# Two gated projections of a decoder block: operand rows requested two groups before their split, additions moved to VectorE, half of the results gated once

## The chip, the cores and the metric

One core of a Trainium2 chip runs the whole program in one launch. The metric is device microseconds of one execution. TensorE (PE) multiplies, ScalarE (ACT) copies, VectorE (DVE) and GpSimd (POOL) work elementwise, SyncE (SP) issues the transfers (DMAs) to and from the chip's memory. Each engine takes its instructions strictly in order: one that waits holds all behind it.

## What is computed

```python
xn = rmsnorm(x, norm1_g[l])
qa, ka, va, qr, kr, vr, gr, gate_a, gate_b = [xn @ wl[:, bounds[i]:bounds[i + 1]] ...]
o_a = ...   # dilated attention, three groups mixed: (1, 1024, 512)
o_r = retention(...)
o_r = head_groupnorm(o_r, ...) * silu(gr)          # (1, 1024, 2048)
y = sigmoid(gate_a) * (o_a @ w_proj_a[l]) + sigmoid(gate_b) * (o_r @ w_proj_b[l])
x = x + y @ w_out[l]
x = x + square(relu(rmsnorm(x, norm2_g[l]) @ w_up[l])) @ w_down[l]
```

The sequence has 1024 rows, the model 1024 columns. The change concerns the end of the retention and the line of `y`: the two products and the two gates.

## The kernel before, in words

All numbers are float32. An operand is split into a high and a low part (`xh`, `xl`; for weights `wh`, `wl`): ACT copies the high part (L320), DVE subtracts it for the low part (L321), and each product of two operands is three matmuls, high by high, high by low, low by high. A group of 12 matmuls (four pieces of the inner dimension, three matmuls each) fills one tile of PSUM with 128x512 results, always issued at L223.

The stages that matter here follow each other on PE:

- **Retention**, four heads of eight chunks. Each chunk's output is normalised (L847 to L854), turned and multiplied by a gate (`turn_o`, L879 to L896); for the second half of the sequence POOL forms sums and differences of row blocks there (L893 to L896), and SP stores them all to `on_d` (L874). In the last four chunks `load_oa` (L802) brings the attention's output in and splits it.
- **The projection of the attention's output**, called `pa` below: 16 groups (eight column blocks `d`, two halves of the sequence), PSUM tile `ms`. A gate tile `s0` is loaded (L929, pool `pm2` of four buffers, three groups ahead), DVE multiplies it with the product (L957), SP stores it to `pa_d` (L958). After each group `load_sum` requests one 512 KB piece of rows of the next projection from `on_d` (L941, tile `oraw`, two buffers) and splits it at once.
- **The sevenfold projection of the retention's output**, called `pb`: eight units, the first four over one half of the inner dimension (c=0), the last four over the other (c=1). A unit computes a 2x2 block of results from seven products N1 to N7 in place of eight (Strassen's scheme), each a group of 12 matmuls; 56 groups in all, PSUM tiles `mm` and `ms`. Its weights are loaded by SP in raw form (L176), summed by DVE (L121) and split. Behind the products stand small steps: N1 is copied with its sign turned (L387, ACT), N6 is copied (L392, ACT), N7 is copied (L395, ACT) and the PSUM tile of N5 subtracted (L396, DVE), N3 is subtracted (L401, DVE). N2, N7, N4 and N3 each end in one result of 128x512, the blocks (0,0), (1,1), (1,0), (0,1) of (`f`, half of the sequence). In units 0 to 5 the order is N7, N4, N3, with products of unit j+2 between them; in units 6 and 7 N3 stands right behind N7 and uses the PSUM bank that L396 reads.
- Each result is multiplied by its gate (L1013, DVE; the gate loaded at L929 as `s1`) and added to what stands in memory (loaded at L929 as `s2`): POOL adds at L1015, L1018 or L1021, except in the last unit, where DVE adds. The added tile comes from `pa_d` in units 0 to 3 and from `pb_d` in units 4 to 7. Units 0 to 3 store to `pb_d` (L1016); units 4 to 7 split their results for the next projection (`keep`, L320/L321) or store them for later (L1022).
- Then the `w_out` projection, the up and the down projection.

What sets the order: the Python program writes all instructions in order, and a scheduler places them on the engines' queues by what they depend on and by when their buffers come free. So a load stands on SP where the program asks for it and its buffer has been released, and a split stands in ACT's and DVE's queue even where its load has not landed.

## Time and profile before

| what | value |
|---|---|
| time, median of 3 runs | 2283.23 us (2280.83 to 2285.7) |
| the profiled execution's own time | 2280.93 us |
| its span on the engines | 2279.2 us |
| mean granted TensorE clock | 0.992 |
| end of the retention, first group of `pa` on PE | 1302.7 us |
| `pa` on PE | 1302.7 to 1367.7 us |
| `pb` on PE | 1367.7 to 1547.6 us |

The span runs from the first to the last instruction of the trace, and all places in time are counted from its start. In the tables of windows each stretch has its length, then for each engine the busy time and the number of instructions, then the granted clock (1.00 is full), the busy share of the DMA engines and the rate. In the timeline a row has start, duration, engine, line, operation and tiles; the bracket at its end is the idle time of that engine before it, and what ended it.

### The profile page before, as it was taken

How to read it: one execution, taken by the hardware profiler on the slowest of the kernel's cores; microseconds unless marked ns; L12 is line 12 of the kernel's file. 1: busy time of each engine (PE TensorE's matmuls, PEld its weight loads, DVE VectorE, ACT ScalarE, POOL GpSimd, SP SyncE). 2: the span in 40 equal slices, each digit the busy share in tenths (PEclk: the TensorE clock that was granted, in tenths of full speed). 3: DMA queues.
4: the chain of work that ended last, by engine and by line, in shares of the span. 5: the costliest groups of instructions: out<-in, count | busy, mean ns of one | idle time of the engine just before them, and what ended most of it. 6: DMA issues, size and time to landing. Idle time of an engine off the chain costs nothing. (4 is left out here: it accounts for less than half of the span.)

```text
span 2279.2 us, 30618 instructions
## 1 busy us (share of the span) xinstructions
PE 2222.4 (98%) x10772; PEld 1898.7 (83%) x10772; DVE 1349.3 (59%) x2531; ACT 1044.1 (46%) x2330; POOL 444.8 (20%) x465
## 2 busy tenths in 40 slices
PE   8999999999999999999999989899999999899999
PEld 7999999998888888888888867677778888688777
DVE  6444545355544445558776756773765556687874
ACT  6444435345333333445555534342555555654542
POOL 1111111110000000002133112220000000587883
PEclk9999999999999999999999999999999999999999
DMA  4313132222233333264454388764345556645432
GB/s 151 95 52 112 56 94 93 82 84 98 88 111 111 111 111 109 100 190 126 116 148 124 118 269 290 264 220 145 118 120 152 153 152 191 221 153 180 163 133 102
DMA packets 248717, 313.74 MB, mean 138 GB/s; under 512 B 15218, under 2 KB 171250, under 8 KB 248563
## 3 DMA queue, kind: packets, MB, share of 16 engines
q1 hardware_dynamic: 248562, 311.79, 42.7%
q8 instruction: 84, 1.38, 0.2%
q14 instruction: 71, 0.57, 0.1%
HBM read 212.02 MB, written 99.71 MB: 137 GB/s over the span
## 5 line engine op out<-in xcount | busy, mean ns | idle before, releaser
L321 DVE TENSOR_TENSOR wl<-raw,wh 128x1024 fp32r<-128x1024 f32 (+2 forms) x290 | 321.6, 1112 | 361.5 <-ACT wh L320 360.6
L223 PE MATMUL mm<-wh,xh 128*128 128x384 f32 (+1 forms) x1226 | 481.7, 393 | 0.6 <-DVE Y L1252 0.5
L223 PE MATMUL mm<-wh,xl 128*128 128x384 f32 (+1 forms) x1226 | 438.8, 358 | 2.2 <-DVE xl L321 2.2
L223 PE MATMUL mm<-wl,xh 128*128 128x384 f32 (+1 forms) x1226 | 437.5, 357 | 0.0
L320 ACT ACTIVATE wh<-raw 128x1024 fp32r<-128x1024 f32 (+2 forms) x290 | 273.5, 945 | 350.6 <-PE ms L223 105.9
L223 PE MATMUL mm<-xh,wh 128*128 128x512 f32 x720 | 284.3, 395 | 18.0 <-ACT ms L387 8.5
L223 PE MATMUL ms<-xh,wh 128*128 128x512 f32 x700 | 277.8, 397 | 9.8 <-DVE s L957 9.2
L223 PE MATMUL mm<-xl,wh 128*128 128x512 f32 x720 | 283.1, 393 | 1.7 <-DVE xl L321 1.7
L223 PE MATMUL mm<-xh,wl 128*128 128x512 f32 x720 | 282.9, 393 | 0.0
L223 PE MATMUL ms<-xl,wh 128*128 128x512 f32 x700 | 274.0, 391 | 0.7 <-DVE xl L321 0.7
L223 PE MATMUL ms<-xh,wl 128*128 128x512 f32 x700 | 273.9, 391 | 0.0
L223 PEld LDWEIGHTS mm<-wh,xl 128*128 128x128 f32 x1226 | 230.7, 188 | 22.4 <-DVE xl L321 3.1
L223 PEld LDWEIGHTS mm<-wh,xh 128*128 128x128 f32 x1226 | 231.8, 189 | 19.9 <-DVE Y L1252 1.3
L223 PEld LDWEIGHTS mm<-wl,xh 128*128 128x128 f32 x1226 | 232.5, 190 | 16.6
L223 PEld LDWEIGHTS mm<-xh,wh 128*128 128x128 f32 x720 | 136.8, 190 | 49.5 <-ACT ms L387 10.0
L223 PEld LDWEIGHTS ms<-xh,wh 128*128 128x128 f32 x700 | 132.6, 189 | 41.0 <-DVE s L957 8.3
L223 PEld LDWEIGHTS mm<-xl,wh 128*128 128x128 f32 x720 | 136.9, 190 | 30.4 <-DVE xl L321 2.1
L223 PEld LDWEIGHTS mm<-xh,wl 128*128 128x128 f32 x720 | 136.8, 190 | 28.8
L223 PEld LDWEIGHTS ms<-xh,wl 128*128 128x128 f32 x700 | 132.2, 189 | 27.9
L223 PEld LDWEIGHTS ms<-xl,wh 128*128 128x128 f32 x700 | 132.4, 189 | 27.5 <-DVE xl L321 1.0
L852 POOL TENSOR_TENSOR st<-st,half 128x1 f32<-128x1 f32 x32 | 25.5, 798 | 647.9 <-DMA sr<-sr_d 489.1
L334 POOL TENSOR_TENSOR ssa<-ssa,half 128x2 f32<-128x2 f32 x96 | 66.5, 693 | 427.6 <-DVE ssa L333 404.7
(301 smaller groups left out, 3698.6 us busy)
## 6 DMA issues: line engine op xcount, KB each, us to landing
raw<-in_w_att SPq DMA_DIRECT2D x48, 384.0 KB, 3.8
raw<-in_w_up SPq DMA_DIRECT2D x32, 512.0 KB, 3.8
h_d<-s SPq DMA_DIRECT2D x64, 256.0 KB, 4.3
raw<-in_w_down SPq DMA_DIRECT2D x32, 512.0 KB, 3.9
oraw<-on_d SPq DMA_DIRECT2D x28, 512.0 KB, 5.4
s<-sg_d SPq DMA_DIRECT2D x48, 256.0 KB, 3.9
xh<-h_d SPq DMA_DIRECT2D x11, 896.0 KB, 4.5
xl<-h_d SPq DMA_DIRECT2D x10, 896.0 KB, 4.7
```

What stands on the lines that cost most here:

```text
L223: self.nc.tensor.matmul(ps, x, y, start=start, stop=stop, skip_group_check=not first)
L320: nc.scalar.activation(dst_h, src, AF.Copy)
L321: nc.vector.tensor_tensor(dst_l, src, dst_h.bitcast(F), op=OP.subtract)
L334: nc.gpsimd.tensor_tensor(dst, dst, half[:, :w], op=OP.pow)
L852: nc.gpsimd.tensor_tensor(st[:, 9:10], st[:, 8:9], half[:, 0:1], op=OP.pow)
```

## The change

In units 0 to 3 results with `f == i` (N2 and N7) are no longer gated: N2 is copied out of PSUM by ACT (L1020), and both are stored to `pb_d` as they are. Their gating is done once in units 4 to 7, as (stored + new) times gate plus `pa`: three DVE instructions (L1025 to L1027) and three loads. The other two results of a unit keep the product with the gate and the addition, now both on DVE (L1029, L1030). So the 29 POOL additions go, and DVE's instructions for results go from 35 to 56; loads of 256 KB go from 32 to 16 in units 0 to 3 and from 32 to 40 in units 4 to 7.

`load_sum` now only requests its rows; the split (`part_sum`) is written two groups later. In `pa` a request is written every second group, in `pb` every group as long as fewer than two are under way. The first three gates and the first three requests are written at the end of the retention, for which their pools are opened inside it. There are 28 requests of rows before and after; 12 stand in `pa` before, 3 in the retention and 7 in `pa` after, where N4 of c=0 moves into `pb`. The results' tiles share one ring of seven buffers (before: three each of `s1` and `s2`). The new lines of the moved steps: split L320/L321 as before, row requests L786, gate loads L779, stores to `on_d` L894, to `pa_d` L963, gating in `pa` L962.

```diff
@@ -771,9 +771,29 @@
     gst.close()
 
 
+    SUMS = ("N1", "N2", "N5", "N4", "N7", "N3", "N6")
+    work = [(d, cs) for d in range(KT) for cs in halves()]
+
+    def loaded(from_, src, name):
+        t = from_.tile([P, 512], F, name=name)
+        nc.sync.dma_start(t, src)
+        return t
+
+    def load_sum(from_, c, name, h):
+
+        raw = from_.tile([P, 2, 512], F, name="oraw")
+        o = 2 * SUMS.index(name)
+        nc.sync.dma_start(raw, on_d[2 * c + h, o:o + 2].rearrange("k p t -> p k t"))
+        return raw
+
+    def part_sum(to, raw, h):
+
+        split(*(x[:, 2 * h:2 * h + 2] for x in to), raw)
+
...
-        cp = pool(ph, "cp2", 1)
+        comb, load = ExitStack(), ExitStack()
+        pc = pool(comb, "pc", 2)
...
         def load_oa(s):
-            raw = p2b.tile([P, S], F, name="oar", bufs=1)
+            raw = pr.tile([P, S], F, name="oraw")
...
-            St = cp.tile([P, 2, DV], F, name="St")
+            St = p2b.tile([P, 2, DV], F, name="St", bufs=1)
...
+                if (h, c) == (2, 1):
+                    comb.close()
+                    pr = pool(load, "pr", 3)
+                    pm2 = pool(load, "pm2", 4)
...
                 if h == RH - 1 and c >= 4:
                     load_oa(c - 4)
...
+                if h == RH - 1 and c == NT - 1:
+                    gates = [loaded(pm2, sg_d[0, d, :, cs], "s0") for d, cs in work[:3]]
+                    raws = [(name, g, load_sum(pr, 0, name, g), -3) for name, g in (("N5", 0), ("N5", 1), ("N7", 0))]
...
-        pr = pool(ph, "pr", 2)
-        load = ExitStack()
-        pm2 = pool(load, "pm2", 4)
-
...
-        gates = [loaded(pm2, sg_d[0, d, :, cs], "s0") for d, cs in work[:3]]
...
-        def load_sum(c, name, h):
-
-            raw = pr.tile([P, 2, 512], F, name="oraw")
-            o = 2 * SUMS.index(name)
-            nc.sync.dma_start(raw, on_d[2 * c + h, o:o + 2].rearrange("k p t -> p k t"))
-            xh, xl = OPB[c][name]
-            split(xh[:, 2 * h:2 * h + 2], xl[:, 2 * h:2 * h + 2], raw)
-
-        waiting = [(name, h) for name in ("N5", "N7", "N1", "N2", "N6", "N4") for h in range(2)]
...
-                if len(gates) < len(work):
-                    e, es = work[len(gates)]
-                    gates.append(loaded(pm2, sg_d[0, e, :, es], "s0"))
-                sga = gates[2 * d + (cs.start > 0)]
-                pp = ms.tile([P, 512], F, name="ms")
-                pipe.step(pp, [(uh[:, k * P:(k + 1) * P], ul[:, k * P:(k + 1) * P], oaS[k][0][:, cs], oaS[k][1][:, cs])
-                               for k in range(SLOTS)], {SLOTS - 1: lambda: W.free(ua)} if cs.start else None)
-                nc.vector.tensor_tensor(sga, sga, pp, op=OP.mult)
-                nc.sync.dma_start(pa_d[d, :, cs], sga)
...
-                if waiting and (ES or waiting[0][0] in OPB[0]):
-                    load_sum(0, *waiting.pop(0))
+        waiting = [("N7", 1)] + [(name, h) for name in ("N1", "N2", "N6") for h in range(2)]
+        for n, (d, cs) in enumerate(work):
+            if not cs.start:
+                ua, = W.take(1)
+                uh, ul = W[ua]
+            if len(gates) < len(work):
+                e, es = work[len(gates)]
+                gates.append(loaded(pm2, sg_d[0, e, :, es], "s0"))
+            pp = ms.tile([P, 512], F, name="ms")
+            pipe.step(pp, [(uh[:, k * P:(k + 1) * P], ul[:, k * P:(k + 1) * P], oaS[k][0][:, cs], oaS[k][1][:, cs])
+                           for k in range(SLOTS)], {SLOTS - 1: lambda: W.free(ua)} if cs.start else None)
+            nc.vector.tensor_tensor(gates[n], gates[n], pp, op=OP.mult)
+            nc.sync.dma_start(pa_d[d, :, cs], gates[n])
...
+            if raws and raws[0][0] in OPB[0] and raws[0][3] <= n - 2:
+                name, h, raw, _ = raws.pop(0)
+                part_sum(OPB[0][name], raw, h)
+            if waiting and waiting[0][0] in OPB[0] and n % 2 and len(raws) < 3:
+                name, h = waiting.pop(0)
+                raws.append((name, h, load_sum(pr, 0, name, h), n))
+        for name, h, raw, _ in raws:
+            part_sum(OPB[0][name], raw, h)
...
-        for h in range(2):
-            load_sum(0, "N3", h)
-            load_sum(1, "N1", h)
-
+        pr = pool(ph, "pr2", 2)
...
-        class parts:
-            @staticmethod
-            def tile(shape, dtype, name):
-                return pub.tile(shape, dtype, name=name, bufs=2 if name == "u2" else 1)
-
-        pm3 = pool(ph, "pm3", 3)
+        pm3 = pool(ph, "pm3", 7)
...
-            src = pa_d if j < 4 else pb_d
-            ahead[results[n]] = loaded(pm3, sg_d[1, d, :, cs], "s1"), loaded(pm3, src[d, :, cs], "s2")
+            if j < 4 and f == i:
+                return
+            srcs = [sg_d[1], pa_d] if j < 4 else [sg_d[1], pb_d] + [pa_d] * (f == i)
+            ahead[n] = [loaded(pm3, src[d, :, cs], "s") for src in srcs]
 
...
-            sgb, y = ahead.pop(results[n])
-            nc.vector.tensor_tensor(sgb, sgb, src, op=OP.mult)
+            if n not in ahead:
+                y = src
+                if src.space == PSUM:
+                    y = pm3.tile([P, 512], F, name="s")
+                    nc.scalar.activation(y, src, AF.Copy)
+                nc.sync.dma_start(pb_d[2 * j + f, :, cs], y)
+                return
+            sgb, y, *pa = ahead.pop(n)
+            if pa:
+                nc.vector.tensor_tensor(y, y, src, op=OP.add)
+                nc.vector.tensor_tensor(y, y, sgb, op=OP.mult)
+                nc.vector.tensor_tensor(y, y, pa[0], op=OP.add)
+            else:
+                nc.vector.tensor_tensor(sgb, sgb, src, op=OP.mult)
+                nc.vector.tensor_tensor(y, y, sgb, op=OP.add)
             if j < 4:
-                nc.gpsimd.tensor_tensor(y, y, sgb, op=OP.add)
                 nc.sync.dma_start(pb_d[2 * j + f, :, cs], y)
             elif f or cs.start:
-                (nc.vector if j == 7 else nc.gpsimd).tensor_tensor(y, y, sgb, op=OP.add)
                 keep(j, f, cs, y)
             else:
-                nc.gpsimd.tensor_tensor(y, y, sgb, op=OP.add)
                 nc.sync.dma_start(yl_d[j - 4], y)
 
...
-        todo, unit = [], {}
+        todo, unit = [(c, name, h) for c, name in ((0, "N4"), (0, "N3"), (1, "N1")) for h in range(2)], {}
...
-        for j, name in order:
-            product("pb", j, name, unit, OPB[j // 4], lambda: parts, result)
-            todo += [(new, h) for new in after.get((j, name), ()) for h in range(2)]
-            if todo:
-                load_sum(1, *todo.pop(0))
+        for i, (j, name) in enumerate(order):
+            product("pb", j, name, unit, OPB[j // 4], lambda: pub, result)
+            todo += [(1, after[j, name], h) for h in range(2) if (j, name) in after]
+            if begun and begun[0][0] <= i - 2:
+                _, c, op, h, raw = begun.pop(0)
+                part_sum(OPB[c][op], raw, h)
+            if todo and len(begun) < 2:
+                begun.append((i, *todo[0], load_sum(pr, *todo.pop(0))))
...
```

PE's rows stand in the same order before and after. Three places of the other queues follow; numbers behind names are those of buffers.

**SP in the middle of `pa`** (`pa_d` is the store of a gated result, `s0` the load of a gate, `oraw` the request of rows, `on_d` the stores of the last chunks of the retention). Before:

```order
L958 DMA pa_d_87<-s0_12843 128x512
L941 DMA oraw_13002<-on_d_85 128x2x512
L874 DMA on_d_85<-onE_12619 128x4x128
L929 DMA s0_13006<-sg_d_82 128x512
L874 DMA on_d_85<-onT_13023 128x4x128
L874 DMA on_d_85<-n6_13029 128x2x128
L176 DMA raw2_13044<-in_w_pb_q 128x1024
L958 DMA pa_d_87<-s0_12845 128x512
L941 DMA oraw_13066<-on_d_85 128x2x512
L958 DMA pa_d_87<-s0_12920 128x512
L929 DMA s0_13070<-sg_d_82 128x512
L941 DMA oraw_13087<-on_d_85 128x2x512
```

The same place after the change:

```order
L963 DMA pa_d_87<-s0_12842 128x512
L894 DMA on_d_85<-n6_12993 128x2x128
L894 DMA on_d_85<-onE_12526 128x4x128
L894 DMA on_d_85<-onT_12987 128x4x128
L779 DMA s0_13008<-sg_d_82 128x512
L963 DMA pa_d_87<-s0_12851 128x512
L894 DMA on_d_85<-onE_12626 128x4x128
L894 DMA on_d_85<-onT_13025 128x4x128
L894 DMA on_d_85<-n6_13031 128x2x128
L176 DMA raw2_13046<-in_w_pb_q 128x1024
L779 DMA s0_13072<-sg_d_82 128x512
L963 DMA pa_d_87<-s0_12924 128x512
```

The requests of rows between the gates and stores are gone from this stretch; the stores to `on_d` still stand between the gate loads.

**ACT in the last chunks of the retention** (`wh5` is a weight of `pa`, `vh`, `smh` and `Sh` belong to the retention's chunks, `on` is a chunk's output). Before:

```order
L320 ACTIVATE wh0_12733<-raw0_11932 128x512
L884 ACTIVATE onT_12719<-tr_12714,gng_105 128x128 x4
L320 ACTIVATE wh1_12764<-raw1_11960 128x512
L847 ACTIVATE on_12755<-ms_12745 128x512
L320 ACTIVATE Sh_12783<-St_11991 128x512
L320 ACTIVATE wh3_12792<-raw2_11985 128x512
L320 ACTIVATE Sh_12783<-St_11991 128x512
L320 ACTIVATE wh5_12817<-raw0_12737 128x512
L320 ACTIVATE vh_12823<-mm_12707 128x512
L320 ACTIVATE smh_12806<-sm_12804 128x128
```

After:

```order
L320 ACTIVATE wh0_12740<-raw0_11939 128x512
L320 ACTIVATE wh1_12771<-raw1_11967 128x512
L320 ACTIVATE xh_96<-oraw_12846 128x1024
L867 ACTIVATE on_12762<-ms_12752 128x512
L320 ACTIVATE xh_98<-oraw_12848 128x1024
L320 ACTIVATE Sh_12790<-St_11998 128x512 x2
L320 ACTIVATE wh3_12799<-raw2_11992 128x512
L320 ACTIVATE wh5_12824<-raw0_12744 128x512
L320 ACTIVATE vh_12830<-mm_12714 128x512
L320 ACTIVATE xh_98<-oraw_12968 128x1024
L904 ACTIVATE onT_12865<-tr_12860,gng_105 128x128 x2
L320 ACTIVATE smh_12813<-sm_12811 128x128
```

Four splits of requested rows (`xh<-oraw`) now stand between the chunks' steps, and `wh5` of `pa` stands ahead of `vh` and `smh` as before.

**ACT at unit 3 of `pb`** (L387 is the copy of an N1, L395 that of an N7, `wh` are weights). Before:

```order
L320 ACTIVATE xh_13064<-oraw_13905 128x1024
L320 ACTIVATE wh2_13887<-raw1_13661 128x1024
L392 ACTIVATE u2_13903<-ms_13627 128x512
L320 ACTIVATE xh_13064<-oraw_13922 128x1024
L320 ACTIVATE xh_96<-oraw_13941 128x1024
L387 ACTIVATE ms_13939<-mm_13926 128x512
L320 ACTIVATE wh5_13967<-raw0_13659 128x1024
L395 ACTIVATE u3_13957<-ms_13627 128x512
```

After:

```order
L320 ACTIVATE xh_13066<-oraw_13876 128x1024
L392 ACTIVATE u2_13874<-ms_13605 128x512
L320 ACTIVATE wh2_13858<-raw1_13635 128x1024
L320 ACTIVATE xh_13066<-oraw_13891 128x1024
L387 ACTIVATE ms_13906<-mm_13893 128x512
L320 ACTIVATE xh_96<-oraw_13910 128x1024
L320 ACTIVATE wh0_13940<-raw1_13938 128x1024
L395 ACTIVATE u3_13924<-ms_13605 128x512
L320 ACTIVATE wh5_13932<-raw0_13633 128x1024
```

Ahead of the copy at L387 stood the splits of two pieces of rows, of which one now stands behind it; in the program the request of each is written two groups ahead.

**DVE at the results of units 4 and 5.** Before:

```order
L396 TENSOR_TENSOR u3_14278<-u3_14278,mm_14234 128x512
L321 TENSOR_TENSOR xl_13056<-s1_14247,xh_13055 128x512
L1013 TENSOR_TENSOR s1_14179<-s1_14179,u3_14278 128x512
L1013 TENSOR_TENSOR s1_14206<-s1_14206,mm_14249 128x512
L321 TENSOR_TENSOR xl_95<-s2_14181,xh_94 128x512
L321 TENSOR_TENSOR wl4_13279<-raw2_14140,wh4_13278 128x512
L1013 TENSOR_TENSOR s1_14281<-s1_14281,ms_13939 128x512
```

After:

```order
L396 TENSOR_TENSOR u3_14258<-u3_14258,mm_14214 128x512
L1025 TENSOR_TENSOR s_14186<-s_14186,mm_14229 128x512
L1025 TENSOR_TENSOR s_14157<-s_14157,u3_14258 128x512
L1026 TENSOR_TENSOR s_14186<-s_14186,s_14184 128x512
L1026 TENSOR_TENSOR s_14157<-s_14157,s_14155 128x512
L1027 TENSOR_TENSOR s_14186<-s_14186,s_14188 128x512
L1027 TENSOR_TENSOR s_14157<-s_14157,s_14159 128x512
L321 TENSOR_TENSOR xl_13058<-s_14227,xh_13057 128x512
L321 TENSOR_TENSOR wl4_13265<-raw2_14115,wh4_13264 128x512
L321 TENSOR_TENSOR xl_95<-s_14157,xh_94 128x512
```

Six instructions for two results of three steps each stand in one row behind L396, where one product each stood before.

More of the change, by code (lines that the diff above doesn't have):

```diff
@@ new lines, in hybrid_block @@
+        waiting = [("N7", 1)] + [(name, h) for name in ("N1", "N2", "N6") for h in range(2)]
[11 more added lines that the diff above has]
+            nc.sync.dma_start(pa_d[d, :, cs], gates[n])
+            if ES is None and not pipe.due:
+                ret.close()
+                more = pool(body, "more", 1, "right")
+                W.more = more
+                ext = pool(exts, "ext", 3, "right")
+                ES = [slot_of(ext) for _ in range(3)] + [slot_of(pool(e1, "ext1", 1, "right"))]
+                OPB[0].update({"N1": ES[0], "N2": ES[1], "N6": ES[3], "N4": ES[2], "N3": XS[0, 0]})
+                OPB[1].update({"N1": XS[1, 0], "N2": ES[0], "N6": ES[1], "N5": ES[3], "N7": XS[0, 1],
+                               "N4": XS[1, 1], "N3": ES[2]})
+            if raws and raws[0][0] in OPB[0] and raws[0][3] <= n - 2:
[4 more added lines that the diff above has]
+                raws.append((name, h, load_sum(pr, 0, name, h), n))
@@ L1041, in hybrid_block @@
                 u = fetched[j, name]
-                late[u] = loaded(pm3, yl_d[u - 4], "s1")
-        assert not todo and not late
+                late[u] = loaded(pm3, yl_d[u - 4], "s")
+        assert not todo and not begun and not late
         e1.close()
```

27 lines of the change are left out of this document (4 added, 23 removed).

## The prediction

> **What bounds the kernel now.** I read the table of windows first, for the stretch that the change touches and for a calm one as a yardstick.
>
> ```profile
> 1180.00:1300.00 120.00, 119.38 (x580) 98.79 (x579) 86.89 (x186) 65.06 (x137) 25.04 (x32) 1.00 0.38 112
> 1560.00:1600.00 40.00, 40.00 (x179) 33.11 (x178) 9.65 (x11) 9.04 (x19) 0.00 (x0) 1.00 0.37 126
> 1300.00:1548.00 248.00, 220.47 (x917) 177.08 (x916) 169.68 (x207) 95.60 (x128) 61.93 (x45) 0.94 0.76 251
> ```
>
> The second row gives the price of a matmul where PE never waits and the clock is full: 40.00/179 = 0.2235 us, so 2.68 us for a group of twelve. At that price the 917 matmuls of the third row are 204.9 us; the stretch took 248. So 43 us, 1.9% of the whole time, is lost here: PE was idle 27.5 us, and the rest went in matmuls that ran longer, at a mean clock of 0.94. The first row, the retention just before, has almost no idle PE. Everything that this change can win lies in the third row.
>
> Who ends the idle time, from the view of waits of PE over the third row's stretch (releaser, total us, count, longest):
>
> ```profile
> PE ms L223 <- DVE s L957: 9.2, 5, 5.7
> PE mm L223 <- ACT ms L387: 8.5, 3, 7.0
> PE mm L223 <- DVE u L396: 7.3, 2, 4.5
> PE mm L223 <- DVE s L1013: 2.1, 1, 2.1
> ```
>
> Four lines hold 27.1 of the 27.5 us: the gating in `pa`, the copy of an N1 on ACT, the subtraction behind N7, and one gating in `pb`. A stall also costs clock, seen in the slices of 20 us that hold or follow the long ones:
>
> ```profile
> 1340.00:1360.00 20.00, 12.89 (x41) 10.06 (x42) 8.70 (x9) 6.17 (x6) 0.00 (x0) 0.74 0.85 275
> 1380.00:1400.00 20.00, 17.90 (x72) 14.35 (x71) 12.15 (x14) 9.17 (x12) 5.91 (x4) 0.91 0.85 298
> 1460.00:1480.00 20.00, 20.00 (x78) 16.26 (x79) 15.41 (x19) 8.78 (x11) 7.80 (x4) 0.87 0.71 243
> 1520.00:1540.00 20.00, 15.50 (x60) 12.33 (x60) 13.39 (x16) 8.45 (x12) 5.04 (x3) 0.91 0.74 239
> ```
>
> I count the cost as busy time less matmuls at 0.2235 us: 12.89 - 41 x 0.2235 = 3.7 us in the first slice, 17.90 - 16.1 = 1.8 in the second, 20.00 - 17.4 = 2.6 in the third, 15.50 - 13.4 = 2.1 in the fourth.
>
> **Why `pa` waits.** The longest wait at L957, followed back through the timelines of PE, DVE, SP and POOL:
>
> ```profile
> 1331.27 0.73 POOL L895 TENSOR_TENSOR onE<-onE,n 128x256 f32<-128x256 f32 x1
> 1332.03 0.36 SPq L874 DMA_DIRECT2D on_d<-onE  x1
> 1334.83 0.45 SPq L958 DMA_DIRECT2D pa_d<-s  x1
> 1340.41 0.32 SPq L929 DMA_DIRECT2D s<-sg_d  x1
> 1344.46 0.69 DVE L957 TENSOR_TENSOR s<-s,ms 128x512 f32<-128x512 f32 x1 [0.47 <-DMA s<-sg_d]
> 1345.21 0.79 PE L223 MATMUL ms<-xh,wh 128*128 128x512 f32 x1 [5.67 <-DVE s L957]
> ```
>
> SP stood at a store of the retention until POOL's subtraction ended at 1332.00, so the store of a gated result left only at 1334.83. Its buffer came free when that landed; the next gate's load followed at 1340.41 and landed as DVE began at 1344.46. The table of DMA issues gives the two flights (last number, us from issue to landing) and that of the rows:
>
> ```profile
> s<-sg_d SPq DMA_DIRECT2D x48, 256.0 KB, 3.9
> pa_d<-s SPq DMA_DIRECT2D x16, 256.0 KB, 5.4
> oraw<-on_d SPq DMA_DIRECT2D x28, 512.0 KB, 5.4
> ```
>
> One buffer is held for load, product and store, 3.9 + 0.69 + 5.4 = 10.0 us; with four buffers that is one group per 2.5 us, and PE needs one per 2.68. There is almost nothing to spare, so any delay on SP reaches PE.
>
> **Why `pb` waits.** The longest wait at L387:
>
> ```profile
> 1448.87 1.96 POOL L1015 TENSOR_TENSOR s<-s,s 128x512 f32<-128x512 f32 x1 [4.50 <-DMA s<-pa_d]
> 1450.86 0.32 SPq L1016 DMA_DIRECT2D pb_d<-s  x1
> 1451.70 0.45 SPq L941 DMA_DIRECT2D oraw<-on_d  x1
> 1458.21 1.06 ACT L320 ACTIVATE xh<-oraw 128x1024 fp32r<-128x1024 f32 x1 [8.35 <-DMA oraw<-on_d]
> 1459.17 0.58 ACT L387 ACTIVATE ms<-mm 128x512 f32<-128x512 f32 x1
> 1459.81 0.80 PE L223 MATMUL mm<-xh,wh 128*128 128x512 f32 x1 [7.01 <-ACT ms L387]
> ```
>
> The store waits for POOL's slow addition, the request of rows stands behind it on SP, and ACT stands 8.35 us at the split of those rows while the copy that PE needs is queued behind. The last kind, at L396, is different:
>
> ```profile
> 1518.88 0.63 ACT L320 ACTIVATE xh<-s 128x512 fp32r<-128x512 f32 x1 [0.94 <-POOL s L1018]
> 1522.36 0.50 PE L223 MATMUL mm<-xh,wh 128*128 128x512 f32 x1 [4.49 <-DVE u L396]
> 1537.67 1.06 ACT L320 ACTIVATE wh<-raw 128x1024 fp32r<-128x1024 f32 x1 [1.31 <-PE ms L223]
> 1538.64 0.58 ACT L395 ACTIVATE u<-ms 128x512 f32<-128x512 f32 x1
> 1538.76 1.23 DVE L321 TENSOR_TENSOR wl<-raw,wh 128x1024 fp32r<-128x1024 f32 x1 [1.14 <-ACT wh L320]
> 1539.90 0.68 DVE L396 TENSOR_TENSOR u<-u,mm 128x512 f32<-128x512 f32 x1
> 1540.64 0.79 PE L223 MATMUL mm<-xh,wh 128*128 128x512 f32 x1 [2.78 <-DVE u L396]
> ```
>
> In units 6 and 7 N3 follows N7 at once and needs the bank that L396 reads, behind a weight split. That is 2.78 us, and it stays, since this order is unchanged; the other wait of 4.49 had a POOL addition in its chain besides.
>
> **The change part by part.** All against the profiled execution's 2280.93 us.
>
> *Requests in `pa`.* At stake are 9.2 us of waits and 3.7 of clock, 12.9. Requests fall from twelve to seven here, and the DMAs (busy 0.85 in the slice) carry less beside the gates. But the chain of 10.0 us on four buffers stays as it is, and SP still stands at `on_d` stores between the gate loads, as the order shows. I take a little over half: **+7** (0 to +12.9).
>
> *The same work in the retention.* Four splits move there: on ACT 4 x 1.06 = 4.2 us, on DVE 4 x 1.23 = 4.9 us. The first window has both engines with room on average (65.06 and 86.89 of 120), but at the retention's end the chunks' steps stand behind them in ACT's row, as does the weight `wh5`; the requests of such weights
>
> ```profile
> 1295.80 2.34 SPq L176 DMA_DIRECT2D raw<-in_w_pa  x2
> ```
>
> left before the last stores, and I expect them behind some of these now. Bounds: nothing, and all 4.9 on the path. I take the middle, **-2.5**, as a stall near 1311.
>
> *Requests in `pb` and no POOL additions.* At stake are 8.5 + 2.1 us of waits and 2.6 + 1.8 of clock, 15.0. The store that held SP for POOL now waits for DVE. A request leads its split by two groups, 2 x 2.68 = 5.4 us, and the flight is 5.4: just enough, nothing to spare. So most goes, and one or two waits of 1 to 1.5 us with their clock stay: **+11** (0 to +15.0).
>
> The Trainium skill, "TensorE: Matmul & The Clock Gate", section "Part 1: The HAM clock gate", has the clock fall to half after an idle window of about 3.4 us and rise again after as long a busy one. By that rule the 2.10 us wait in `pb` would have cost no clock, and the 1.8 us counted for it would not be there to win: the sum would be about 1.3 us less, 2269. The slice 1380 to 1400 with its 0.91 speaks against it, so I keep the measured 1.8.
>
> *Waits at L396.* The part above the inherent one goes with POOL: 4.49 - 2.78 = **+1.7** (0 to +1.7).
>
> *Additions on DVE.* DVE's instructions for results go from 35 to 56. From the groups of DVE and of POOL in `pb`:
>
> ```profile
> L1013 DVE TENSOR_TENSOR s<-s,u 128x512 f32<-128x512 f32 x16 | 11.0, 686 | 0.1
> L121 DVE TENSOR_TENSOR raw<-raw,raw 128x512 f32<-128x512 f32 x14 | 13.5, 964 | 0.2
> L121 DVE TENSOR_TENSOR raw<-raw 128x512 f32<-128x512 f32 x13 | 10.8, 834 | 0.1
> ```
>
> 21 x 0.686 = 14.4 us more. The same shape takes 964 and 834 ns at L121, where POOL runs beside it; if these fall to 686, 14 x 0.278 + 13 x 0.148 = 5.8 us come back. The net 8.6 us lies in DVE's free 78 us of the third window, unless it bunches. The row that decides is the busiest slice in which PE did not wait:
>
> ```profile
> 1480.00:1500.00 20.00, 20.00 (x90) 16.57 (x89) 15.70 (x18) 8.61 (x12) 5.87 (x4) 1.00 0.77 266
> ```
>
> DVE 15.70 of 20 is 14.8 us per unit of 7 x 2.68 = 18.8. Units 4 and 5 get six more instructions, 4.1 us, and lose 2 x 0.278 + 2 x 0.148 = 0.85: 18.0 of 18.8 us. It fits barely. I take **-2** (0 to -8.6).
>
> *The rest at nothing:* four copies of N2 on ACT (4 x 0.58 = 2.3 us if on the path; ACT is busy 95.60 of 248), and 2 MB fewer transfers.
>
> Sum: 7 - 2.5 + 11 + 1.7 - 2 = 15.2 us less, so 2265.7 on the scale of the profiled execution. That one lies 2.3 below the median of the runs; on the median's scale **2268**.
>
> **The rivals.**
>
> *The flights still bound.* The gate chain (2.5 of 2.68 us per group) gives nothing back as soon as one store hangs on SP, and a flight of 5.4 us behind a lead of 5.4 leaves ACT waiting. For it: both margins are a few tenths. Against: fewer requests share the DMAs. With `pa` at 0 and half of `pb`, 0 - 2.5 + 5.5 + 1.7 - 2 = 2.7 us, so 2280.5; with less lost, up to 2275.
>
> *DVE becomes the bound, slower than before.* At 18.0 of 18.8 us per unit, another 0.8 us decides. Then L396 comes late in every unit as it does now in the last two, since it stands among six result instructions, and N7's bank is held. Six more units pay 2.8 us and a clock loss of 2.1 as in the slice from 1520: 6 x 4.9 = 29 us, against the 15.5 that the first three terms win: 14 us slower, 2297. For it: the durations of the last row. Against: successive instructions overlap a little (1538.76 to 1539.90 is 1.14 for a 1.23 us one), and units 0 to 3 add almost nothing. If only units 4 and 5 pay, the gain shrinks by 9.8 and stays.
>
> *It does not do what it says.* In `pb` two buffers of rows are left, and a request waits for the split two before it; the lead may exist in the written order only. Then only the small terms remain, -2.5 + 1.7 - 2, 2286 at worst, about 2283 with the POOL hold gone.
>
> **How the numbers follow.** Forecast as above, gain 8 to 24, 2259 to 2275: 0.54. Better still: 0.05. Flights still bound, 2275 to 2281: 0.17, half of it beyond 0.2%, which is about what a measurement can tell from no change (4.6 us). No real lead, about 2283: 0.06. DVE bound, 2286 to 2297: 0.18. Faster 0.05 + 0.54 + 0.09 = 0.68, same 0.08 + 0.06 = 0.14, slower 0.18. The range 2259 to 2288 leaves out the better case and most of the DVE case.
>
> **What would show it.** Right, if in the waits of PE the lines L387 and L1013's successors (L1025, L1029) fall under 3 us together, L396 stays at two waits near 2.8, the gating in `pa` (now L962) keeps 2 to 5 us, and a new short stall stands near 1311. Wrong, if DVE's busy share in units 4 and 5 passes 0.95 with waits at L396 there, if ACT still stands at `xh<-oraw` for 4 us or more in `pb`, or if the gate loads in `pa` still come after a store's landing with PE behind them.

## The result: 2265.3 us against 2283.4, and the profile after

The changed kernel takes 2265.27 us (median of 4 runs, 2263.69 to 2266.03), the one before 2283.41 in the same runs: a ratio of 0.992 (95% interval 0.9903 to 0.9937). The forecast was 2268, the range 2259 to 2288. The two profiled spans, 2279.2 and 2262.8 us, differ by 16.4 us, and the steps below are made against these.

The waits of PE after, first in the retention's end and `pa`, then in `pb` (releaser, total us, count, longest):

```profile
PE ms L223 <- DVE St L886: 1.6, 1, 1.6
PE tr L899 <- DVE on L874: 1.5, 1, 1.5
PE ms L223 <- ACT on L867: 0.2, 1, 0.2
```

```profile
PE mm L223 <- DVE u L396: 5.7, 2, 2.8
PE mm L223 <- ACT ms L387: 3.1, 2, 2.5
PE ms L223 <- ACT u L395: 2.6, 2, 2.1
PE ms L223 <- ACT u L392: 1.1, 1, 1.1
```

The gating of `pa` (L962 now) is in neither list: its 9.2 us are gone altogether. In `pb` 18.2 us became 12.5, and two lines are new, the copies of N7 and N6 on ACT. The retention's end has 3.3 us that it did not have before.

The slices that hold the longer waits:

```profile
1300.00:1320.00 20.00, 16.70 (x68) 12.82 (x67) 15.21 (x32) 8.97 (x17) 7.34 (x9) 0.91 0.70 216
1340.00:1360.00 20.00, 20.00 (x89) 16.47 (x89) 11.74 (x16) 5.45 (x7) 0.00 (x0) 1.00 0.91 298
1360.00:1380.00 20.00, 17.49 (x70) 13.94 (x69) 15.88 (x17) 12.49 (x15) 0.00 (x0) 0.91 0.84 289
1460.00:1480.00 20.00, 17.28 (x75) 13.64 (x74) 15.58 (x23) 7.87 (x11) 0.00 (x0) 1.00 0.78 265
1500.00:1520.00 20.00, 15.31 (x67) 11.98 (x65) 14.90 (x20) 9.14 (x12) 0.00 (x0) 1.00 0.78 258
1520.00:1540.00 20.00, 19.02 (x71) 15.54 (x72) 11.11 (x16) 4.71 (x7) 0.00 (x0) 0.83 0.35 122
```

Counted as in the prediction (busy time less matmuls at 0.2235 us), the first slice lost 16.70 - 15.2 = 1.5 us to the clock, the third 17.49 - 15.6 = 1.9, the last 19.02 - 15.9 = 3.1. The slice 1340 to 1360, which had a clock of 0.74 before, runs at 1.00.

What DVE does in `pb`, by windows of the whole stage, before and then after, and by groups, after:

```profile
1367.00:1548.00 181.00, 162.80 (x678) 131.57 (x678) 130.64 (x148) 71.37 (x91) 48.08 (x29) 0.94 0.75 251
```

```profile
1357.00:1530.00 173.00, 160.39 (x678) 129.70 (x678) 130.27 (x171) 73.63 (x94) 0.00 (x0) 0.97 0.74 247
```

```profile
L321 DVE TENSOR_TENSOR wl<-raw,wh 128x1024 fp32r<-128x1024 f32 x27 | 32.7, 1221 | 18.0 <-ACT wh L320 17.9
L321 DVE TENSOR_TENSOR xl<-oraw,xh 128x1024 fp32r<-128x1024 f32 x18 | 22.0, 1221 | 16.9 <-ACT xh L320 15.6 <-PE ms L223 1.3
L121 DVE TENSOR_TENSOR raw<-raw,raw 128x512 f32<-128x512 f32 x16 | 10.8, 683 | 0.1
L121 DVE TENSOR_TENSOR raw<-raw 128x512 f32<-128x512 f32 x16 | 10.8, 682 | 0.0
```

In the two windows the third busy time, DVE's, is the one to compare: 130.64 us in 148 instructions before, 130.27 in 171 after. The instructions that came cost nothing in sum, because those that were there run faster without POOL beside them: the sums of weights fell from 964 and 834 ns to 683 and 682, and the splits, which the profile of before shows as

```profile
L321 DVE TENSOR_TENSOR wl<-raw,wh 128x1024 fp32r<-128x1024 f32 x25 | 33.3, 1339 | 9.9 <-ACT wh L320 9.8
L321 DVE TENSOR_TENSOR xl<-oraw,xh 128x1024 fp32r<-128x1024 f32 x16 | 21.7, 1365 | 22.9 <-ACT xh L320 22.9
```

from 1339 and 1365 ns to 1221. The run adds_dve below, which moves the additions and nothing else, shows the same: 682 and 684 ns for the sums, 1220 and 1221 for the splits. The Trainium skill, "SBUF — State Buffer", section "Who interferes with whom", says that a VectorE instruction with two inputs in SBUF contends with a GpSimd instruction that reads SBUF, for a port pair that one of them holds exclusively. These rows agree with it.

The longest new wait in `pb` apart from L396 and the start is one at the copy of N7. From the timelines of SP, ACT and PE after:

```profile
1459.24 0.38 SPq L786 DMA_DIRECT2D oraw<-on_d  x1
1465.43 1.06 ACT L320 ACTIVATE xh<-oraw 128x1024 fp32r<-128x1024 f32 x1 [2.59 <-DMA oraw<-on_d]
1466.39 0.58 ACT L395 ACTIVATE u<-ms 128x512 f32<-128x512 f32 x1
1467.02 0.50 PE L223 MATMUL ms<-xh,wh 128*128 128x512 f32 x1 [2.10 <-ACT u L395]
```

The rows were 6.2 us on the way (1459.24 to 1465.43), longer than the 5.4 of two groups. But ACT had stood at the split for 2.59 us, so it came there at 1462.84, only 3.6 us behind the request. It is the same kind of wait as before at L387, 2.10 us in place of 7.01.

### The profile page after: what moved, and what is told of

Its sections match the earlier page's. It is cut to its first block, busy times and chain, and to the rows that moved or that the text cites. A ratio compares the mean times of both kernels' runs of the same rounds, so it can differ in the third digit from the quotient of the medians.

```text
span 2262.8 us, 30601 instructions
## 1 busy us (share of the span) xinstructions
PE 2217.5 (98%) x10772; PEld 1897.1 (84%) x10772; DVE 1349.2 (60%) x2552; ACT 1046.1 (46%) x2334; POOL 399.4 (18%) x436
## 5 line engine op out<-in xcount | busy, mean ns | idle before, releaser
L321 DVE TENSOR_TENSOR wl<-raw,wh 128x1024 fp32r<-128x1024 f32 (+2 forms) x290 | 318.3, 1101 | 368.8 <-ACT wh L320 367.8
L320 ACT ACTIVATE wh<-raw 128x1024 fp32r<-128x1024 f32 (+2 forms) x290 | 273.3, 945 | 348.3 <-PE ms L223 116.3
L223 PEld LDWEIGHTS mm<-wh,xl 128*128 128x128 f32 x1226 | 230.7, 188 | 21.9 <-DVE xl L321 2.7
L223 PEld LDWEIGHTS mm<-xl,wh 128*128 128x128 f32 x720 | 136.3, 189 | 30.2 <-DVE xl L321 2.2
L872 POOL TENSOR_TENSOR st<-st,half 128x1 f32<-128x1 f32 x32 | 27.5, 858 | 646.7 <-DVE st L871 641.4
```

The lines of the kernel that those rows point to most:

```text
L223: self.nc.tensor.matmul(ps, x, y, start=start, stop=stop, skip_group_check=not first)
L320: nc.scalar.activation(dst_h, src, AF.Copy)
L321: nc.vector.tensor_tensor(dst_l, src, dst_h.bitcast(F), op=OP.subtract)
L872: nc.gpsimd.tensor_tensor(st[:, 9:10], st[:, 8:9], half[:, 0:1], op=OP.pow)
```

## The experiments

Twelve kernels, each in five rounds beside the kernel before. Ratios are to that kernel on the same chip, with 95% intervals; 0.2% is 4.6 us. Waits are PE's in the profile.

**adds_dve.** The kernel before with the additions alone moved:

```diff
-                nc.gpsimd.tensor_tensor(y, y, sgb, op=OP.add)
+                nc.vector.tensor_tensor(y, y, sgb, op=OP.add)
...
-                (nc.vector if j == 7 else nc.gpsimd).tensor_tensor(y, y, sgb, op=OP.add)
+                nc.vector.tensor_tensor(y, y, sgb, op=OP.add)
```

> The kernel before with nothing changed but the place of the additions of the results: DVE in place of POOL. Theory (two sources: in pa the requests of rows, in pb the POOL additions that held SP): the waits of PE in pa stay near 9 us, those at L387 and at the gating of pb fall from 10.6 us to under 4, and the time falls by about 7 us to 2276. Rival 1 (all comes from the lead of the requests): within 2 us of before, 2283, the wait at L387 still over 7 us. Rival 2 (all comes from POOL): about 2267.

Measured: 2276.25 against 2285.23, ratio 0.9966 (0.9956 to 0.9975).

```profile
PE ms L223 <- DVE s L957: 8.8, 4, 5.3
PE ms L223 <- ACT u L395: 7.0, 2, 4.4
PE mm L223 <- DVE u L396: 5.7, 2, 2.8
PE mm L223 <- ACT ms L387: 2.2, 3, 0.9
PE mm L223 <- DVE s L1013: 1.7, 1, 1.7
```

The waits at L387 and L1013 fell to 3.9 us and `pa` kept its 8.8, and the time came out, as the theory of two sources had it. But 7.0 us turned up at L395, so that all waits in `pb` fell only from 18.2 to 16.6 us: ACT still stands at late rows (37.4 us of its waits in `pb`, 22.8 before), only with another copy behind them.

**lead_only.** The kernel after with results, additions on POOL and buffers for results as before:

```diff
-            if j < 4 and f == i:
-                return
-            srcs = [sg_d[1], pa_d] if j < 4 else [sg_d[1], pb_d] + [pa_d] * (f == i)
-            ahead[n] = [loaded(pm3, src[d, :, cs], "s") for src in srcs]
+            src = pa_d if j < 4 else pb_d
+            ahead[n] = loaded(pm3, sg_d[1, d, :, cs], "s1"), loaded(pm3, src[d, :, cs], "s2")
...
+            nc.vector.tensor_tensor(sgb, sgb, src, op=OP.mult)
...
+                nc.gpsimd.tensor_tensor(y, y, sgb, op=OP.add)
```

> The kernel after, with the results as before: every result gated, additions on POOL, three buffers each for gates and sums; so only the requests of rows are changed. Theory (two sources): no wait in pa (9.2 us and 3.7 of clock gone), about 3.3 us of waits and 1.5 of clock at the end of the retention, and pb still with 8 us or more of waits at ACT's copies and the gating, since SP still stands at stores that wait for POOL: 2275. Rival 1 (all from the lead): 2267. Rival 2 (all from POOL): 2283.

Measured: 2287.0 against 2285.23, ratio 1.0015 (1.0005 to 1.0024). All three expectations missed. In `pa` no wait is left, as expected, but in `pb`, from 1358 us on:

```profile
PE ms L223 <- ACT u L395: 11.2, 4, 3.8
PE mm L223 <- ACT ms L387: 6.9, 4, 2.1
PE mm L223 <- DVE u L396: 5.7, 2, 2.8
PE ms L223 <- ACT u L392: 2.5, 1, 2.5
```

That is 26.3 us in place of 18.2. `pb` begins at 1358.8 on PE, 8.9 us earlier than before, and ends at 1551.8, 4.2 later: what `pa` gained was given back one stage later. The kernel is not quite the requests alone: the copy of N6 (`u2`) keeps the one buffer of the kernel after, where the kernel before has two, and ACT stands 20.3 us at L392 until DVE's L1015 has released it, which it does not in the kernel before. no_half below has the same one buffer without the loss.

**half_only.** The kernel before with the half gating, the remaining additions on POOL, a ring of seven and one buffer for N6's copy:

```diff
-        pm3 = pool(ph, "pm3", 3)
+        pm3 = pool(ph, "pm3", 7)
...
+            if n not in ahead:
+                y = src
...
+                nc.vector.tensor_tensor(y, y, sgb, op=OP.mult)
+                (nc.vector if j == 7 else nc.gpsimd).tensor_tensor(y, y, pa[0], op=OP.add)
```

> The kernel before with only the gating once of half of the results; all additions that remain on POOL, one ring of seven buffers and one buffer for the copy of N6 as after. Theory (two sources): 21 additions on POOL in place of 29 and none in the results with f == i of units 0 to 3, so one or two of the SP holds go: 2280, with pa unchanged at 9 us of waits. Rival 1 (all from the lead): 2283. Rival 2 (all from POOL): the gain in proportion to the additions, 8 of 29 of 18 us: 2278.

Measured: 2279.44 against 2285.23, ratio 0.9982 (0.9971 to 0.9992). `pa` keeps 10.0 us of waits; in `pb` 17.5 us are left of 18.2 (L396 5.7, L387 5.6, L395 4.5, L392 1.7). A small gain, near what two of the theories said, so it does not separate them. PE's waits are in sum those of before (27.5 us), so they do not account for the gain.

**after_pool.** The kernel after with the last addition of each result on POOL:

```diff
-                nc.vector.tensor_tensor(y, y, pa[0], op=OP.add)
+                (nc.vector if j == 7 else nc.gpsimd).tensor_tensor(y, y, pa[0], op=OP.add)
...
-                nc.vector.tensor_tensor(y, y, sgb, op=OP.add)
+                (nc.vector if j == 7 else nc.gpsimd).tensor_tensor(y, y, sgb, op=OP.add)
```

> The kernel after with only the last addition of each result of L1027 and L1030 on POOL (21 additions; the last unit on DVE as in before). Theory (two sources): pa without waits as after, pb with 5 us more waits than after, at ACT's copies behind late rows: 2271. Rival 1 (all from the lead): 2266. Rival 2 (all from POOL): 2278.

Measured: 2270.04 against 2285.23, ratio 0.9938 (0.9926 to 0.995). The theory of two sources had 2271; `pb` has 15.5 us of waits in place of 12.5, 3 more and not 5, and `pa` has 1.4. Against lead_only, on the same chip, it is 17.0 us faster (2270.04 and 2287.0), and only the half gating with its ring of seven buffers differs: with additions on POOL the half gating is worth much once the requests are early.

**no_half.** The kernel after without the half gating, every result multiplied and added on DVE, three buffers each; it is lead_only with the engine of the additions changed, here at one of the three places:

```diff
-                nc.gpsimd.tensor_tensor(y, y, sgb, op=OP.add)
+                nc.vector.tensor_tensor(y, y, sgb, op=OP.add)
```

> The kernel after without the half gating: every result is multiplied with its gate and added on DVE, with three buffers each for gates and sums as before. The run with the requests alone gave 2287 with 26 us of waits in pb, the one with the additions on POOL and the half gating 2270. Theory (it is the POOL additions that hold SP; the gating of half counts little): 2267, waits at ACT's copies in pb under 9 us. Rival (the 16 gate and sum loads fewer in units 0 to 3 and the ring of seven free SP): 2276, with 15 us or more at ACT's copies.

Measured: 2265.05 against 2283.95, ratio 0.9909 (0.9895 to 0.9922), the same as the whole change within the intervals. Its waits in `pb`:

```profile
PE mm L223 <- DVE u L396: 5.7, 2, 2.8
PE ms L223 <- ACT u L395: 4.6, 3, 3.6
PE mm L223 <- ACT ms L387: 3.1, 1, 3.1
PE ms L223 <- ACT u L392: 0.6, 1, 0.6
```

So the half gating adds nothing that shows once the additions are on DVE. Against lead_only only the engine of the additions differs, and that is worth 1.0107 in ratio (1.0015/0.9909), some 24 us; in the kernel before the same step was worth 0.34%.

**no_early.** The kernel after with the first gates and rows written behind the retention, and rows requested in every group:

```diff
-                if h == RH - 1 and c == NT - 1:
-                    gates = [loaded(pm2, sg_d[0, d, :, cs], "s0") for d, cs in work[:3]]
-                    raws = [(name, g, load_sum(pr, 0, name, g), -3) for name, g in (("N5", 0), ("N5", 1), ("N7", 0))]
...
+        gates = [loaded(pm2, sg_d[0, d, :, cs], "s0") for d, cs in work[:3]]
+        raws = []
+        waiting = [(name, h) for name in ("N5", "N7", "N1", "N2", "N6") for h in range(2)]
...
-            if waiting and waiting[0][0] in OPB[0] and n % 2 and len(raws) < 3:
+            if waiting and waiting[0][0] in OPB[0] and n < 14 and len(raws) < 3:
```

> The kernel after, but the first three gates and rows are requested after the retention's last chunk, and the rows of pa then in every group (ten requests in fourteen groups) with the split two groups later. Theory (pa is cured by the lead, the early part costs): the stalls at the retention's end (3.3 us and 1.5 of clock) go, and pa has under 3 us of waits: 2262. Rival 1 (pa is cured because the early part thins the requests out): 9 us of waits in pa and 4 of clock, 2273.

Measured: 2267.73 against 2283.95, ratio 0.9924 (0.9912 to 0.9936). `pa` has 0.4 us of waits, but the retention's end keeps 1.5 and 1.6 us. The experiment did not do what it was made for: the scheduler put the first four row splits at the same places of ACT's queue inside the retention as in the kernel after, since their buffers are free there. Where the program writes the first requests makes no difference; where the pools are opened may. The denser requests did not come about either: SP issues 7 in `pa`, as in the kernel after, where the kernel before issues 11, and none between 1318 and 1340 us. So the run separates neither the early requests nor their number.

**gates_early.** So the opposite: the kernel before with nothing but the pool moved, requests and splits still together.

```diff
+                if (h, c) == (2, 1):
+                    comb.close()
+                    pm2 = pool(load, "pm2", 4)
...
-            St = cp.tile([P, 2, DV], F, name="St")
+            St = p2b.tile([P, 2, DV], F, name="St", bufs=1)
...
-        pr = pool(ph, "pr", 2)
-        load = ExitStack()
-        pm2 = pool(load, "pm2", 4)
+        pr = pool(load, "pr", 2)
...
         load.close()
+        pr = pool(ph, "pr2", 2)
```

> The kernel before with one part of the change: the buffers of the combination are given back in the retention, and the pool of the gates of pa is opened there. Requests and splits stay together, two buffers for rows in pa and two new ones in pb; results and additions as before. The scheduler then places four gate loads and the first rows in the retention, though the program asks for them behind it. Theory (memory that is free early cures pa, not the written lead): under 2 us of waits at the gating of pa, 3 us of stalls at the end of the retention, pb as before with 18 us of waits: 2275. Rival (the lead of two groups and fewer requests cure pa): 6 us or more at the gating of pa, 2282.

Measured: 2290.13 against 2284.46, ratio 1.0019 (1.0009 to 1.003).

```profile
PE mm L223 <- ACT ms L387: 15.5, 3, 7.8
PE mm L223 <- DVE u L396: 7.3, 2, 4.5
PE ms L223 <- ACT u L395: 5.2, 3, 3.4
PE ms L223 <- ACT u L392: 2.2, 1, 2.2
...
PE ms L223 <- DVE s L958: 0.5, 1, 0.5
```

The gating of `pa` (L958 here) falls from 9.2 to 0.5 us with no lead at all: memory that is free early suffices for `pa`. It thins the requests too, though: SP issues 8 in `pa`, none between 1317 and 1340 us. The time of 2275 was wrong, as in lead_only: the first four lines are `pb`, 30.2 us in place of 18.2. SP's longest waits for POOL's additions in `pb` went from 43.7 us (22.7 at the store, 21.0 at loads) to 55.0 (33.1 and 21.9). `pb` runs from 1359.9 to 1556.3 on PE.

**late_pools.** The kernel no_early with the pools opened behind the retention and one buffer for the attention's rows:

```diff
-            raw = pr.tile([P, S], F, name="oraw")
+            raw = p2b.tile([P, S], F, name="oar", bufs=1)
...
-                    pr = pool(load, "pr", 3)
-                    pm2 = pool(load, "pm2", 4)
...
+        pr = pool(load, "pr", 3)
+        pm2 = pool(load, "pm2", 4)
```

> The kernel after with the pools of gates and rows opened behind the retention, and the attention's rows loaded through one buffer as before; lead, additions and half gating as after. In the order the rows still stand in the retention, the gate loads behind its stores. Theory (the early gates cure pa): 6 us or more of waits at the gating of pa and 3 of clock, 2273. Rival (the rows out of the way cure pa): under 2 us there, and 2265. The stalls of 1.5 and 1.6 us at the retention's end: gone if the attention's three buffers caused them, the same if the four row splits did.

Measured: 2269.59 against 2284.46, ratio 0.9939 (0.9926 to 0.9952); the profiled execution, with a span of 2274.4 us, is the longest of its runs. In the order the first rows stand in the retention, the gate loads behind it. One wait is back at the gating, and the retention's stalls are unchanged:

```profile
PE ms L223 <- DVE s L961: 3.4, 1, 3.4
PE ms L223 <- DVE St L886: 1.6, 1, 1.6
PE tr L899 <- DVE on L874: 1.5, 1, 1.5
```

That is between the two expectations for `pa`: late gates bring back one wait of five. The attention's three buffers are not what stalls the retention's end, since they are gone here; the four row splits remain, here and in every kernel with that stall.

**early_dve.** The kernel gates_early with all additions on DVE, as in adds_dve; neither lead nor half gating.

```diff
-                nc.gpsimd.tensor_tensor(y, y, sgb, op=OP.add)
+                nc.vector.tensor_tensor(y, y, sgb, op=OP.add)
```

> The run with the gates' pool opened in the retention, with the additions on DVE besides: neither the lead of two groups nor the half gating. Theory (two things make the gain: memory that is free early for pa, and no POOL addition in pb): no wait over 1 us at the gating of pa, pb no longer than the 176 us that the additions on DVE alone gave, so 2268. Rival (in pb the lead is needed once pa ends early, as that stage grew by 16 us with the early gates): pb of 185 us or more, 2277.

Measured: 2274.73 against 2282.98, ratio 0.9965 (0.9951 to 0.9978), between the two expectations.

```profile
PE mm L223 <- ACT ms L387: 8.1, 2, 7.8
```

`pa` has 1.5 us at the gating, but the start of `pb` one wait of 7.8. There ACT stood at rows that were requested at 1365.55 and split at 1371.23:

```profile
1365.55 0.37 SPq L942 DMA_DIRECT2D oraw<-on_d  x1
1371.23 1.06 ACT L320 ACTIVATE xh<-oraw 128x1024 fp32r<-128x1024 f32 x1 [4.33 <-DMA oraw<-on_d]
...
1375.86 0.80 PE L223 MATMUL mm<-xh,wh 128*128 128x512 f32 x1 [7.80 <-ACT ms L387]
```

In the kernel after, the wait at the same place is 2.51 us. So early memory and DVE's additions make only part of the gain: no_half, which has the separate requests as well, is at 0.9909. It also has a third buffer for early rows and one buffer less for N6's copy, so that the rest is the lead's is likely, not shown.

**lead_one.** The kernel after with the split in `pb` one group behind its request:

```diff
-            if begun and begun[0][0] <= i - 2:
+            if begun and begun[0][0] <= i - 1:
```

> The kernel after with the splits in pb one group after their request in place of two; pa as after. Theory (a request lands about 5 us after issue, so two groups just cover it): ACT stands some 2.7 us longer at most of the 18 splits, and the waits at its copies in pb go from 6.8 us to 15 or more: 2278. Rival (when SP is not held, the place of the split counts little, since ACT has time to spare): 2267.

Measured: 2267.73 against 2283.95, ratio 0.9926 (0.9915 to 0.9938). Waits in `pb` 15.0 us (L396 5.7, L387 5.0, L395 3.2, L392 1.1), 2.5 more than after; at ACT's copies 9.3 in place of 6.8, where 15 or more were expected. The rival was right: one group or two in the written program differ little.

**swap67** and **weave67.** Two tries at the waits at L396. In both N4 comes ahead of N3 in units 6 and 7; weave67 also puts N6 of unit 7 between N7 and N4 of unit 6.

```diff
-            order += [(j, name) for name in (("N4", "N3") if j < 6 else ("N3", "N4"))]
+            order += [(j, name) for name in ("N4", "N3")]
```

```diff
-            order += [(j, "N6"), (j, "N5"), *more_n[:1], (j, "N7"), *more_n[1:]]
+            more_n = [(7, "N6")] if j == 6 else more_n
+            order += [(j, "N6")] * (j < 7) + [(j, "N5")]
+            order += [(j, "N7"), *more_n] if j > 5 else [*more_n[:1], (j, "N7"), *more_n[1:]]
```

> The kernel after with N4 ahead of N3 in units 6 and 7, as in the other units. Theory (the two waits at L396 come from N3 needing the bank that DVE reads behind a weight split): N4 needs only ACT's copy of N7, so two waits of about 1.6 us at L395 replace 5.7 us, and the half clock behind them (3 us) goes: 2260. Rival (the next product waits for the same weight split on DVE whichever comes first): 2265, with 5 to 6 us of waits there.

> The kernel after with N4 ahead of N3 in units 6 and 7, and N6 of unit 7 between N7 and N4 of unit 6, as units 0 to 5 have a product of a later unit there. Theory (a product in between hides the copy of N7): only unit 7 waits at that copy, 2.6 us or less, and 2259. Rival (unit 7's weights come too late for the earlier place): a new wait of 2 us or more at a weight split, 2263.

Measured: swap67 2260.91 against 2283.95, ratio 0.9903 (0.989 to 0.9916); weave67 2263.89 against 2284.46, ratio 0.9908 (0.9895 to 0.9921). In swap67, from the waits of the whole stretch:

```profile
PE ms L223 <- ACT u L395: 7.9, 5, 2.6
```

The line of L396 is gone from both. In its place swap67 waits 1.47 and 2.65 us at L395, weave67 1.31 at L392 and 2.38 at L395. swap67 is near its theory, 2260; weave67 missed its 2259, with a wait at L392 that neither expectation had and none at a weight split. Both ratios are lower than that of the change, by 3.9 and 2.7 us, but the intervals overlap its own (0.9903 to 0.9937): a gain over it is not shown. Neither was tried together with no_half.

## Why the prediction came out right, step by step

The total was right, 15.2 us less against 16.4 in the profiled spans. The terms were not all, and that they made up for each other is luck: `pa` gave 5.9 us more and DVE 2 more than forecast, the retention's end 2.3 and `pb` 4.4 less. Of the signs named, L396 kept its two waits of 2.84 us and the new stalls stand near 1311, but the gating in `pa` kept none of the 2 to 5 us and L387 kept 3.1, not under 3. ACT's longest wait for rows in `pb` is 3.8 us, where 4 or more were named as a sign of being wrong.

- **`pa`: +7 forecast, +12.9 measured.** All 9.2 us of waits and the 3.7 of clock went. The step that failed is the chain of 10.0 us on four buffers, which was to stay as it is. The table of DMA issues after has the store at 3.9 us in place of 5.4:

```profile
pa_d<-s SPq DMA_DIRECT2D x16, 256.0 KB, 3.9
```

  With 4.1 us for the gate loads (median of all 40 in the kernel) that makes 4.1 + 0.69 + 3.9 = 8.7 us, one group per 2.2. It is not the whole cause: early_dve, with stores of 5.3 us, has 1.5 us of waits. The DMAs were not freer in the slice from 1340 (0.91, before 0.85). gates_early shows that opening the pools inside the retention suffices, without a lead. But the forecast's reason, fewer requests, is not refuted: the kernels with 8.8 us or more of these waits (before, adds_dve, half_only) issue 11 requests of rows in `pa`, all others 7 or 8. With four gates in place before `pa` begins, the stage starts with its buffers full; late_pools, with the gates late, has one wait of 3.4 us again. How the 9.2 us divide between early gates and fewer requests is open.
- **The retention's end: -2.5 forecast, -4.8 measured** (3.3 us of waits and 1.5 of clock). The mechanism was right and the place near (1304 and 1312, forecast 1311), the size at the far end of the bounds; what ran on the path was DVE's splits, as this stretch of the timelines after shows:

```profile
1297.74 1.75 DVE L321 TENSOR_TENSOR xl<-oraw,xh 128x1024 fp32r<-128x1024 f32 x1
1301.40 1.21 DVE L321 TENSOR_TENSOR xl<-oraw,xh 128x1024 fp32r<-128x1024 f32 x1
1301.56 1.46 POOL L872 TENSOR_TENSOR st<-st,half 128x1 f32<-128x1 f32 x1 [0.76 <-DVE st L871]
1303.78 0.54 DVE L874 TENSOR_SCALAR on<-on,st 128x512 f32<-128x512 f32 x1
1304.47 0.63 PE L899 MATMUL tr<-ident,on 128*128 128x128 f32 x4 [1.54 <-DVE on L874]
```

  The first split lasted 1.75 us in place of 1.23 and held the chunk's statistics; the second ran beside POOL's short step of the normalisation, 1.46 us here and 0.55 before, which comes before L874. Every kernel with these splits has the stalls, and the three without (before, adds_dve, half_only) have none, but no run took out the splits alone.
- **`pb`, ACT's queue and SP: +11 forecast, about +6.6 measured.** Waits apart from L396 went from 10.9 to 6.8 us and their clock from 4.4 to 1.9. The premise that failed is the lead of 5.4 us. With requests and splits of rows paired in order, ACT reached 13 of the 18 splits of `pb` less than 5.4 us behind their request, the one at 1459 after 3.6. So a part of the rival "it does not do what it says" came true: the two groups are there in the written order, and less on the chip, which fits lead_one. The rival of the flights had its share too (6.2 us at 1459). One wait, 1.1 us at L392, comes from DVE: ACT waits there for L1029 to release the one buffer that N6's copy now has.
- **L396: +1.7 forecast, +1.6 measured** in waits, as reasoned. Of the clock, 3.8 us were lost there before (2.1, and 1.7 in the slice 1540 to 1560) and 3.1 after, another 0.7.
- **Additions on DVE: -2 forecast, no loss measured.** The stage's DVE time is the same (130.64 and 130.27 us). The relief was mis-sized: it was counted at L121 alone, and the splits at L321 got faster too. DVE's busiest slice of the stage has 17.32 of 20 us, where 19.2 of 20 follows from the 18.0 of 18.8 forecast:

```profile
1480.00:1500.00 20.00, 18.92 (x84) 15.35 (x83) 17.32 (x27) 8.43 (x13) 0.00 (x0) 1.00 0.72 236
```

  So the rival of a bound DVE fell short, with its mechanism seen only in the 1.1 us at L392.

Sum of the measured terms: 12.9 - 4.8 + 6.6 + 1.6 + 0.7 = 17.0, against 16.4; the rest lies in the stages behind.

What adding terms hid is that they depend on each other. The requests without the other two parts (lead_only) made the kernel slower, 1.0015; additions alone gave 0.9966, half gating alone 0.9982. Requests and additions together give 0.9909, far more than their product of 0.9981; requests and half gating, with the 21 additions that it leaves on POOL (after_pool), give 0.9938. So behind early requests either of the other two parts brings most of the gain, and both together no more than one (0.992).

In lead_only and gates_early, with all 29 additions on POOL, an earlier end of `pa` was worth nothing. SP's waits for POOL in `pb`, all together, move the same way: 47.5 us before, 56.8 and 58.9 in these two, 33.3 in after_pool. Why `pb` then loses 8 to 12 us of waits more than before, and not just as much, is open: no run took apart SP's waits, the transfers beside them and, in lead_only, the one buffer of N6's copy.

## What to carry to other kernels

Price a change in one stage together with the stage that starts earlier because of it: two kernels here lost all of a gain of 8 to 9 us one stage later. Parts of a change can also stand in for each other: try each with the others in place, not only alone. Where a scheduler hoists loads, it is the moment at which their memory comes free that sets when they run, not the line at which they are written. Moving elementwise work from POOL to DVE cost DVE nothing here, since its other instructions ran faster without POOL beside them (683 ns in place of 964); compare the stage's busy time, not the count of instructions.

## What was not expected of the hardware

- DVE's sums of two SBUF tiles took 964 ns with POOL's additions in the stage and 683 without; splits of 128x1024 took 1339 and 1221.
- A stall costs clock in some places and not in others. In the kernel after, the slice with waits of 1.54 and 1.60 us ran at 0.91, the one with 2.10 at 1.00, and of the two waits of 2.84 at L396 the first (slice 1500 to 1520) left 1.00 and the second 0.83 behind it. The Trainium skill, "TensorE: Matmul & The Clock Gate", section "Part 1: The HAM clock gate", has the clock fall after at least one idle window of about 3.4 us, and the window run freely. That a stall's place in such a window decides would fit these rows, but no run shows it; a full idle window is not needed for the loss, as the stalls of 1.54 and 1.60 us show.
